# The mask products of three attentions: issued once per bank of scores and ahead of them, with one set of score products for both branches of the sparse attention

## The chip, the cores and the metric

One core of a Trainium2 chip runs the whole program. The metric is the time on the device, in microseconds; of the kernel before there are three runs, with a median of 2802.47 us (2797.93 to 2806.33).

The core's engines work side by side, each from its own queue: TensorE (PE in the profile; its loads of weights, PEld) multiplies matrices, VectorE (DVE) and ScalarE (ACT) work element by element and reduce, GpSimd (POOL) takes a few such steps, SyncE (SP) issues most of the transfers. TensorE writes to PSUM, eight banks of 128 rows by 512 fp32 numbers. A product there has a stationary operand, which is loaded first, and a moving one, whose columns stream through.

## The reference, cut to what matters

256 tokens of width 1024 pass through two blocks of two layers each. Three of the four mixers are attentions, and a causal mask belongs to each score before its softmax:

```python
# _diff_attention, 8 heads of 2 components, 64 wide
sc = jnp.einsum('bqhcd,bkhcd->bhcqk', qb, kb).astype(f32) * scale
sc = jnp.where(mask, sc, -jnp.inf)
...
# nsa_mixer (sparse attention), 16 heads in 4 key groups: the selected and the window branch
p_s = masked_softmax(s_s.reshape(...), m_s)
p_w = masked_softmax(jnp.einsum('bgrqd,bgkd->bgrqk', qb, kw), m_w)
...
# fox_mixer, 16 heads, with the forget gates' running sums c
s = jnp.einsum('bhqd,bhkd->bhqk', qb, k).astype(jnp.float32) + cb[..., None] - c[:, :, None, :]
p = masked_softmax(s, pos[None, :] <= t[:, None])
```

With 256 tokens, the window and the selected blocks of the sparse attention both cover all keys up to the query, so both branches have the same mask. The other layers (a gated MLP, feed-forward layers, two layers of 16,384 experts each) are dense products with weights that are read once.

## The kernel before, in words

The tokens are two tiles of 128, t = 0 and 1. Products in fp32 are made of three float32r products each: an operand is split into a high and a low part, and `mm3` (lines 254 to 258) adds high by high, low by high and high by low in one accumulation. Weights come in blocks of 128 by 1024: SyncE loads them, ScalarE and VectorE split them (lines 248 and 249), TensorE multiplies (lines 397 and 469 with 512 columns, `lin_b` through `mm3` with 256).

The schedule is written by hand: each engine gets its instructions in the order in which the Python code issues them. In an attention, `attend` (line 899) runs over units. A unit is two sets of scores that share one PSUM bank, each 128 queries by kn keys, where kn is 128 for tile 0 and 256 for tile 1. In the differential attention (`unit`, line 1049) and in fox (`unit`, line 1705) the two sets are two heads, 8 units per tile; in the sparse attention (`nsa`, `unit`, line 1491) they are one head's selected and window branch, 16 units per tile. Each tile has two banks for its scores, used in turn. The parts of a unit trail one another by the steps that `ORDER` (line 50) gives: `scores`; `peak`, the row maxima by VectorE (line 958); `soft`, the exponentials by ScalarE (line 965); `scale`; `turn`, the transposes by TensorE (lines 1098, 1543, 1742) and their split; `pv`, the product with v. So the scores of unit i can only be written once the exponentials of unit i - 2 have been read out of the bank. `weave` (line 911) mixes the units of both tiles with blocks of the product before ("c") and of the one after ("w"), in the order of the strings `FILL` (line 52).

The mask is added by TensorE. `maskb` holds 0 or -1e30 in bfloat16, `identb` the identity; the product of the two, 128 columns, is added to the last 128 keys of each set of scores, after them, and closes the set's accumulation (lines 1064, 1506 and 1723). In the sparse attention the code before is

```python
for b in range(2):
    p = self.A[t].halves[i % 2][:, b * S:b * S + kn]
    self.mm3(p, [x[rr, h // 2, ts_] for x in qT], [x[rr, b, g, :kn] for x in kT], True, False)
    nc.tensor.matmul(p[:, kn - P:], self.identb, self.maskb, start=False, stop=True)
```

The queries are the stationary operand, the keys the moving one; `rr` takes 64 rows, those of one head, so a score product uses 64 of TensorE's 128 rows while the mask product and the transposes use all. In fox a fourth product per set, over 4 rows (line 1722, `cx`), adds the running sums. The maxima of a unit wait for its last product, before the change a mask product.

Of the kernel before, what the change touches and what calls it, by code (L numbers as in the profile page):

```python
# [59 lines left out]
def ffn_ops():  # L60
    """The pairs of up blocks ("u") and the down blocks ("d") in their order."""
    ops = [("u", 4)] + [("d", f) for f in range(4)] + [("u", 5)] + [("d", f) for f in range(4, 8)]
    for k in range(6, 14):
        ops += [("u", k), ("d", 2 * k - 4), ("d", 2 * k - 3)]
    return ops + [("u", 14), ("u", 15)] + [("d", f) for f in range(24, 32)]
# [5 lines left out]
class Stream:  # L71
    """The weights, block by block: a load, then the two float32r parts in a slot."""
# [9 lines left out]
    def aside(self, key):  # L82
        """True for the blocks whose second part GpSimd makes."""
# [8 lines left out]
    def open(self, pool, n):  # L92
        """n more slots, for the blocks that the plan lets use them."""
        self.free += [self._slot(pool, self.k.nm("x"), True) for _ in range(n)]
# [18 lines left out]
    def _one(self):  # L113
        """Splits the next block, if there is room for it."""
# [56 lines left out]
class Wide:  # L171
    """[128, 1024] in two banks of PSUM, of which one can be written while the other is read."""
# [15 lines left out]
class Build:  # L188
# [17 lines left out]
    def tick(self):  # L206
        """One step of each task."""
# [14 lines left out]
    def begin(self, task):  # L222
        """A task whose first step goes out at once."""
# [6 lines left out]
    def need(self, t):  # L230
        """The input of a stage, tile t."""
# [22 lines left out]
    def mm3(self, out, s, m, start, stop):  # L254
        mm = self.nc.tensor.matmul
        mm(out, s[0], m[0], start=start, stop=False)  # L256
        mm(out, s[1], m[0], start=False, stop=False)  # L257
        mm(out, s[0], m[1], start=False, stop=stop)  # L258

    def ps(self, shape):  # L260
        """The next bank of the ring, as a shape."""
# [22 lines left out]
    def rstd(self, ms, eps, table=True, beside=None, r=None):  # L284
        """(ms + eps) ** -0.5, by ScalarE's table or, to leave its tables alone, by GpSimd; ms may be in two parts.

        beside() goes out while it is on its way."""
# [20 lines left out]
    def load_table(self, func):  # L308
        """ScalarE's table of func, ahead of its use."""
# [12 lines left out]
    def transpose_split(self, src, dst, c0, n, tsl, scale=None):  # L322
        """src [128 tokens, n*128]: chunks c0.. of dst[hi/lo][:, c, tsl]."""
# [8 lines left out]
    def wait(self, n):  # L332
        """Steps in which weights aren't split."""
# [5 lines left out]
    def turn_raw(self, t, xt, wait):  # L339
        """h's tile t, transposed and split into xt, without the norm's gain (the weights have it) and its r."""  # L340
# [6 lines left out]
    def turn_normed(self, t, g, xt, wait, table, part):  # L347
        """rmsnorm of h's tile t, transposed and split into xt; the last norm without xt."""
# [11 lines left out]
    def chain(self, t, m, post, pre, xt, wait=5, table=True):  # L360
        """h += m, or its rmsnorm; then the next stage's norm, with its gain pre or raw."""
# [25 lines left out]
    def block(self, key, c, x, t, out, ws, ncols, start, stop):  # L387
        """out[:, n] (tokens of tile t) += x^T w over row chunk c."""
# [13 lines left out]
    def ahead(self, keys, x, after=None, ncols=1024, start=True, stop=True):  # L402
        """Steps of a product for tile 0; those for tile 1 are put off."""
# [14 lines left out]
    def late(self):  # L418
        """The next block put off; False without one."""
# [18 lines left out]
    def linear(self, keys, x, after=None, ncols=1024, start=True, stop=True, lag=LAG, func=None):  # L438
        """A product for both tiles, tile 1 LAG blocks behind; after(t) once tile t is done.

        Towards the end tile 1 falls up to lag blocks behind, to be done beside what follows for tile 0, and func's
        table is loaded."""
# [13 lines left out]
    def lin_b(self, key, x, out):  # L456
        """out [n, tokens] of one block [128, 8, n]."""
# [134 lines left out]
    def open_side(self, n_gain):  # L592
        """What all but the expert layers use besides: a second input, slots of the stream, gains."""
# [7 lines left out]
    def dump(self, stage):  # L601
        """Ends the program after a stage, for tests of a part."""
# [42 lines left out]
    def load_x(self):  # L645
        """The input, the first weights before and between its tiles."""
# [4 lines left out]
    def load_p(self, i, also=None):  # L651
        """The layer's p, transposed, in two parts."""
# [8 lines left out]
    def proj(self, i, c, t, pt, ws):  # L661
        """pp = p w_proj, row chunk c of tile t."""
# [6 lines left out]
    def gmlp(self, xt, yt):  # L669
        nc, tc, a = self.nc, self.tc, self.a  # L670
        with tc.tile_pool(name="gm", bufs=1) as gp:
# [55 lines left out]
            def spatial():  # L727
                """s + b of all groups; u s of tile 0."""
# [46 lines left out]
    def ffn(self, i, xr, xt, also=None):  # L775
        """xr holds the raw input, xt will hold the normed one, xr the next stage's."""
# [72 lines left out]
    def scaled(self, x, t):  # L849
        """x = A[t] times the norm's r."""  # L850
# [3 lines left out]
    def inverse(self, t):  # L854
        """1 / r as a row."""
# [8 lines left out]
    def ple(self, i, xt, nxt):  # L864
# [11 lines left out]
        def mid(t, c):  # L876
            """The bias over r, that the sigmoid's scale takes back."""
# [21 lines left out]
    def attend(self, n, order, **parts):  # L899
        """Steps over n units: each one's parts trail one another, as far as order says.  # L900

        s: the scores; m: their maxima; e: the exponentials; c: the scale; t: the transposes and their first part;
        l: the second one; p: the product with v."""
# [7 lines left out]
    def weave(self, order, units, join, make):  # L911
        """The steps of both tiles' units (0, 1), those of tile 1's product before (c) and of tile 0's after (w).

        join(t) ends what tile t's units need, before the first of them or where order has z (0) or u (1); make begins
        the product after."""
# [39 lines left out]
    def maxima(self, s, n):  # L955
        """The negated row maxima of the score sets s [128, n, kn]."""
# [4 lines left out]
    def exps(self, s, n, kn, e, nm):  # L961
        """e = exp of the score sets s [128, n, kn] plus nm; the rows' sums."""
# [5 lines left out]
    def low(self, parts):  # L968
        """The second part of what the first was copied from."""
# [7 lines left out]
    def normed(self, e, r, kn, engine):  # L977
        """e [128, 2, kn] times r [128, 2]."""
# [1150 lines left out]
```

## Time and profile before

| what | value |
|---|---|
| runs | 2797.93, 2802.47, 2806.33 us (median 2802.47) |
| profiled execution | span 2807.0 us, on one core; nothing else of its time is listed |
| mean granted TensorE clock | 0.964 of full speed |
| TensorE busy | 2721.5 us, 97% of the span |
| VectorE, ScalarE, GpSimd busy | 73%, 48%, 5% |
| DMA | 448 MB, 160 GB/s on average |

The profile tells one execution. It lists the busy time of each engine, groups of instructions with their mean duration, the waits, and a timeline in which each line has a start and a duration. The ends of matmuls are modelled, because they are pipelined: a product's record lasts longer than the distance to the next start, and it is the distances between starts that add up to time. The granted clock is TensorE's, as a share of 2.4 GHz: 1.00 or 0.50 at any moment, and a mean of the two in a stretch.

### The profile page before, as it was taken

To read this page: it belongs to the slowest core of one execution; us is meant where nothing else is said; L and a number is where in the kernel's file an instruction comes from. 1 tells how busy PE (TensorE), PEld (TensorE's weight loads), DVE (VectorE), ACT (ScalarE), POOL (GpSimd) and SP (SyncE) were. 2 spreads that over 40 slices of the span, in tenths; PEclk is the share of its full clock that TensorE was granted. 3 is DMA by queue.
4 is the path that set the end of the run, shared out by engine and by line. 5 is a ranking of instruction groups with operands and counts; after the bars stand their busy time and mean duration, and the time that the engine had idled before them with its cause. 6 is when DMAs were issued, how large, how long until landed. Compare 5 with 4: busy or idle time off the path is not lost.

```text
span 2807.0 us, 44583 instructions
## 1 busy us (share of the span) xinstructions
PE 2721.5 (97%) x17590; PEld 2355.8 (84%) x17590; DVE 2043.0 (73%) x3492; ACT 1337.9 (48%) x2056; POOL 141.0 (5%) x130
## 2 busy tenths in 40 slices
PE   8999999999879999999999999999999999999998
PEld 6789777898657799999977788777899999877887
DVE  5655766656764579988899965455699888899664
ACT  5544654545443444444444454353554444444553
POOL 2200020000122100000000000010000000000000
PEclk9999997999986999999999999997999999999999
DMA  6655551554450146665555576440456655555663
GB/s 209 183 187 187 170 162 55 185 190 147 153 179 9 39 151 188 180 181 173 168 162 169 170 218 196 145 146 29 135 178 185 186 170 171 165 166 172 207 207 118
DMA packets 125237, 448.43 MB, mean 160 GB/s; under 512 B 15058, under 2 KB 15586, under 8 KB 125028
## 3 DMA queue, kind: packets, MB, share of 16 engines
q1 hardware_dynamic: 122404, 437.45, 50.7%
q0 software_dynamic: 2624, 8.14, 1.0%
q8 instruction: 137, 2.24, 0.3%
q14 instruction: 72, 0.59, 0.1%
HBM read 444.49 MB, written 1.05 MB: 159 GB/s over the span
## 4 chain that ended last, share of the span: by engine, by line
PE 32%; issue 31%; DVE 3%; ACT 1%; DMA 1%; POOL 0%; DVEq 0%; POOLq 0%; ACTq 0%
PE A L469 12%; PE B L256 4%; PE B L258 4%; PE B L257 4%; PE A L397 4%; PE B L1953 1%; DVE lob L249 1%; PE A L256 1%; PE A L1722 0%; PE B L1742 0%; PE A L257 0%; PE A L258 0%; PE B L1543 0%; PE A L1723 0%; DMA trir<-in_c_tri 0%
## 5 line engine op out<-in xcount | busy, mean ns | idle before, releaser
L248 ACT CAST hib<-raw 128x1024 fp32r<-128x1024 f32 x519 | 543.3, 1050 | 716.7 <-PE B L258 344.5
L249 DVE TENSOR_TENSOR lob<-raw,hib 128x1024 fp32r<-128x1024 f32 x508 | 618.5, 1220 | 189.9 <-ACT hib L248 189.3
L256 PE MATMUL B<-xa,hib 128*128 128x256 f32 x2096 | 593.1, 283 | 0.0
L257 PE MATMUL B<-xa,lob 128*128 128x256 f32 x2096 | 588.1, 281 | 0.1
L258 PE MATMUL B<-xa,hib 128*128 128x256 f32 x2096 | 587.2, 280 | 0.0
L469 PE MATMUL A<-hib,xa 128*128 128x512 f32 x1440 | 412.7, 400 | 4.9 <-ACT xa L248 4.9
L257 PEld LDWEIGHTS B<-xa,lob 128*128 128x128 f32 x2096 | 394.9, 188 | 1.2 <-DVE lob L249 0.6
L256 PEld LDWEIGHTS B<-xa,hib 128*128 128x128 f32 x2096 | 394.7, 188 | 0.0
L258 PEld LDWEIGHTS B<-xa,hib 128*128 128x128 f32 x2096 | 394.5, 188 | 0.0
L469 PEld LDWEIGHTS A<-hib,xa 128*128 128x128 f32 x1440 | 266.5, 189 | 65.8 <-ACT xa L248 5.2
L249 DVE TENSOR_TENSOR lox<-raw,hix 128x1024 fp32r<-128x1024 f32 x174 | 211.2, 1226 | 130.3 <-ACT hix L248 129.9
L248 ACT CAST hix<-raw 128x1024 fp32r<-128x1024 f32 x192 | 197.7, 1043 | 159.2 <-PE A L469 53.1
L469 PE MATMUL A<-lob,xa 128*128 128x512 f32 x720 | 227.4, 397 | 0.0
L1960 DVE SCALAR_TENSOR_TENSOR H<-B,H 128x512 f32<-128x512 f32 x128 | 169.6, 1328 | 1.0 <-PE B L1953 0.6
L397 PE MATMUL A<-hix,xb 128*128 128x512 f32 (+1 forms) x520 | 161.1, 409 | 4.9 <-DVE nv L252 4.2
L469 PEld LDWEIGHTS A<-lob,xa 128*128 128x128 f32 x720 | 135.6, 188 | 32.7
L469 PE MATMUL A<-hix,xa 128*128 128x512 f32 x480 | 133.3, 395 | 0.0
L252 DVE SCALAR_TENSOR_TENSOR lox<-raw,gcol,hix 128x1024 fp32r<-128x1024 f32 (+1 forms) x75 | 93.2, 1250 | 42.8 <-ACT hix L251 42.7
L397 PE MATMUL A<-hix,xa 128*128 128x512 f32 x400 | 121.3, 405 | 1.1 <-ACT hix L251 1.1
L397 PEld LDWEIGHTS A<-hix,xb 128*128 128x128 f32 x520 | 98.6, 198 | 26.0 <-DVE nv L252 4.8
L469 PEld LDWEIGHTS A<-hix,xa 128*128 128x128 f32 x480 | 90.0, 187 | 22.0
L249 DVE TENSOR_TENSOR xa<-H,xa 128x256 fp32r<-128x256 f32 x256 | 106.7, 420 | 0.9 <-ACT xa L248 0.9
(502 smaller groups left out, 4798.3 us busy)
## 6 DMA issues: line engine op xcount, KB each, us to landing
raw<-in_u SPq DMA_DIRECT2D x256, 512.0 KB, 3.6
raw<-in_v SPq DMA_DIRECT2D x256, 512.0 KB, 3.7
raw<-in_f_w_down SPq DMA_DIRECT2D x64, 512.0 KB, 3.5
raw<-in_w_up SPq DMA_DIRECT2D x48, 512.0 KB, 4.4
raw<-in_l_w_in SPq DMA_DIRECT2D x40, 512.0 KB, 3.6
raw<-in_b_w_qkv SPq DMA_DIRECT2D x24, 512.0 KB, 4.5
raw<-in_a_w_in SPq DMA_DIRECT2D x16, 512.0 KB, 4.2
raw<-in_f_w_up SPq DMA_DIRECT2D x16, 512.0 KB, 3.6
```

Of the source, the lines that this page charges most:

```text
L248: nc.scalar.copy(hi, src)
L249: engine.tensor_tensor(lo, src, hi.bitcast(F32), op=ALU.subtract)
L252: nc.vector.scalar_tensor_tensor(lo, src, scale, hi.bitcast(F32), op0=ALU.mult, op1=ALU.subtract)
L256: mm(out, s[0], m[0], start=start, stop=False)
L257: mm(out, s[1], m[0], start=False, stop=False)
L258: mm(out, s[0], m[1], start=False, stop=stop)
L397: self.nc.tensor.matmul(out[:, n0:n0 + n], xs[u], w[v][:, n0:n0 + n], start=start and i == 0, stop=stop and i == 2)
L469: self.nc.tensor.matmul(self.A[t][:, n0:n0 + 512], x[u][:, ts_], w[v][:, n0:n0 + 512], start=first and q == 0, stop=last and q == 2)
L1953: nc.tensor.matmul(p[:, t, :], A[:, t].rearrange("p a b -> p (a b)"), B[q][:, t].rearrange("p a b -> p (a b)"), start=q == 0, stop=q == 1)
L1960: nc.vector.scalar_tensor_tensor(hv, p, 1.0 / G_SCALE, hv, op0=ALU.mult, op1=ALU.mult)
```

## The change

A helper `masked` adds the mask to both sets of a bank in one product of 256 columns: its moving operand is `maskb` read twice, and its output is the last 128 keys of both sets. It is issued ahead of the unit's score products, and it, no longer the first score product, starts the accumulation. The score products only add; the last of them ends the unit. In the sparse attention one `mm3` takes the keys of both branches at once, 2 kn columns instead of kn, so that there are three score products in a unit instead of six. In fox the two products with the running sums come right behind the mask, ahead of both heads' scores. The number of mask products falls from 32 to 16 in the differential attention, from 64 to 32 in the sparse one and from 32 to 16 in fox. Comments are dropped as well.

```diff
-    def mm3(self, out, s, m, start, stop):
+    def mm3(self, out, s, m, start, stop, **kw):
...
+    def masked(self, sets):
+        kn = sets.shape[2]
+        self.nc.tensor.matmul(sets[:, :, kn - P:], self.identb, self.maskb[:, None, :].to_broadcast([P, 2, P]),
+                              start=True, stop=False, skip_group_check=True)
...
                 def scores(i):                                  # differential attention
                     r = slice(i % 2 * 64, i % 2 * 64 + 64)
+                    self.masked(banks[i % 2][:, :, :kn])
                     for e in range(2):
                         h = i // 2 * 2 + e
-                        p = banks[i % 2][:, e]
-                        self.mm3(p[:, :kn], [x[r, h, ts_] for x in qkT[0]], [x[r, h, :kn] for x in qkT[1]], True,
-                                 False)
-                        nc.tensor.matmul(p[:, kn - P:kn], self.identb, self.maskb, start=False, stop=True)
+                        self.mm3(banks[i % 2][:, e, :kn], [x[r, h, ts_] for x in qkT[0]],
+                                 [x[r, h, :kn] for x in qkT[1]], False, True, skip_group_check=True)
...
                     rr = slice((h % 2) * 64, (h % 2) * 64 + 64)  # sparse attention
-                    for b in range(2):
-                        p = self.A[t].halves[i % 2][:, b * S:b * S + kn]
-                        self.mm3(p, [x[rr, h // 2, ts_] for x in qT], [x[rr, b, g, :kn] for x in kT], True, False)
-                        nc.tensor.matmul(p[:, kn - P:], self.identb, self.maskb, start=False, stop=True)
+                    self.masked(sets(i))
+                    self.mm3(sets(i), [x[rr, h // 2, ts_] for x in qT], [x[rr, :, g, :kn] for x in kT], False, True,
+                             skip_group_check=True)
...
                     r = slice(64 * b, 64 * b + 64)               # fox
+                    self.masked(banks[b][:, :, :kn])
+                    for e in range(2):
+                        h = 2 * (i // 2 * 2 + e) + b
+                        k4 = 32 * (h // 4 % 2 * 2 + b)
+                        k4, sl = slice(k4, k4 + 4), h // 8 * 2 + e
+                        mm(banks[b][:, e, :kn], cx[k4, 0, sl, ts_], cx[k4, 1, sl, :kn], start=False, stop=False,
+                           skip_group_check=True)
                     for e in range(2):
                         g = i // 2 * 2 + e
-                        h = 2 * g + b
-                        o = banks[b][:, e, :kn]
-                        k4 = 32 * (h // 4 % 2 * 2 + b)
-                        k4, sl = slice(k4, k4 + 4), h // 8 * 2 + e
-                        self.mm3(o, [x[r, g, ts_] for x in qT], [x[r, g, :kn] for x in kT], True, False)
-                        mm(o, cx[k4, 0, sl, ts_], cx[k4, 1, sl, :kn], start=False, stop=False)
-                        mm(o[:, kn - P:], self.identb, self.maskb, start=False, stop=True)
+                        self.mm3(banks[b][:, e, :kn], [x[r, g, ts_] for x in qT], [x[r, g, :kn] for x in kT], False,
+                                 True, skip_group_check=True)
```

## Rows read from the trace of the kernel before

**Rows 1.** Page: busy time, share of the span, instructions, of each engine.

```profile
PE 2721.5 (97%) x17590; PEld 2355.8 (84%) x17590; DVE 2043.0 (73%) x3492; ACT 1337.9 (48%) x2056; POOL 141.0 (5%) x130
```

**Rows 2.** Windows: span, busy (count) of PE, PEld, DVE, ACT, POOL; granted clock, DMA.

```profile
415.00:456.00 41.00, 37.38 (x153) 30.70 (x153) 23.90 (x65) 15.24 (x55) 7.05 (x5) 0.50 0.09 26
829.00:903.00 74.00, 68.49 (x305) 56.81 (x304) 40.16 (x103) 27.54 (x99) 20.06 (x22) 0.56 0.10 35
903.00:950.00 47.00, 43.96 (x309) 36.51 (x308) 26.56 (x71) 25.25 (x83) 14.51 (x16) 1.00 0.00 1
1903.00:1941.00 38.00, 38.00 (x142) 28.98 (x142) 18.83 (x43) 13.81 (x51) 2.35 (x1) 0.51 0.04 15
```

**Rows 3.** Waits of PE in 829 to 952 us: total us, times, longest.

```profile
PE A L256 <- ACT e L965: 3.2, 3, 1.2
```

**Rows 4.** PE timeline, sparse attention, tile 0: start, duration, line, operands.

```profile
861.92 0.47 PE L256 MATMUL A<-nkT,xa 64*128 64x128 f32 x1
862.19 0.42 PE L257 MATMUL A<-nkT,xa 64*128 64x128 f32 x1
862.41 0.41 PE L258 MATMUL A<-nkT,xa 64*128 64x128 f32 x1
862.75 0.29 PE L1506 MATMUL A<-maskb,identb 128*128 128x128 bf16 x1
862.97 0.47 PE L256 MATMUL A<-nkT,xa 64*128 64x128 f32 x1
...
863.89 0.64 PE L1531 MATMUL B<-ident,scr 128*128 128x128 f32 x2
```

**Rows 5.** The same timeline, tile 1 (256 columns), the unit before.

```profile
859.60 0.58 PE L256 MATMUL A<-nkT,xa 64*128 64x256 f32 x1
859.98 0.41 PE L257 MATMUL A<-nkT,xa 64*128 64x256 f32 x1
...
860.76 0.58 PE L256 MATMUL A<-nkT,xa 64*128 64x256 f32 x1
```

**Rows 6.** PE timeline, 512 columns in the differential attention.

```profile
410.68 1.05 PE L397 MATMUL A<-lox,xb 128*128 128x512 f32 x2
411.53 0.66 PE L397 MATMUL A<-hix,xb 128*128 128x512 f32 x2
```

**Rows 7.** PE timeline: the product with v, then scores.

```profile
865.82 0.41 PE L258 MATMUL B<-pt,nv 128*128 128x256 f32 x1
866.16 0.47 PE L256 MATMUL A<-nkT,xa 64*128 64x128 f32 x1
```

**Rows 8.** PE timeline, full clock: a unit of tile 0.

```profile
914.32 0.32 PE L256 MATMUL A<-nkT,xa 64*128 64x128 f32 x1
...
915.51 0.39 PE L1543 MATMUL B<-ident,e 128*128 128x128 f32 x2
```

**Rows 9.** PE groups by shape, 903 to 950 us: count, busy, mean ns.

```profile
L258 PE MATMUL A<-nkT,xa 64*128 64x256 f32 x18 | 5.1, 284 | 0.0
...
L258 PE MATMUL A<-nkT,xa 64*128 64x128 f32 x6 | 1.6, 272 | 0.0
```

**Rows 10.** PE timeline, fox, tile 1.

```profile
1929.16 0.58 PE L256 MATMUL A<-fkT,xa 64*128 64x256 f32 x1
...
1930.10 0.57 PE L1722 MATMUL A<-fcx 4*128 4x256 f32 x1
1930.60 0.29 PE L1723 MATMUL A<-maskb,identb 128*128 128x128 bf16 x1
1930.82 0.58 PE L256 MATMUL A<-fkT,xa 64*128 64x256 f32 x1
```

**Rows 11.** PE groups by shape, 1903 to 1941 us.

```profile
L1722 PE MATMUL A<-fcx 4*128 4x256 f32 x12 | 6.9, 575 | 0.0
```

**Rows 12.** PE groups by shape, 415 to 456 us.

```profile
L256 PE MATMUL A<-qk,qk 64*128 64x256 f32 x14 | 8.0, 574 | 0.0
```

**Rows 13.** PE, split moving operand: count, ns min/median/max, first, last start.

```profile
L258 PE MATMUL B<-gvn,ws x8: 281/283/283, 67.8 to 70.3; 128*128 128x256 f32 x8
```

More of the change, by code (lines that the diff above doesn't have):

```diff
@@ L252, in split @@
             nc.vector.scalar_tensor_tensor(lo, src, scale, hi.bitcast(F32), op0=ALU.mult, op1=ALU.subtract)
-    def mm3(self, out, s, m, start, stop):
+    def mm3(self, out, s, m, start, stop, **kw):
         mm = self.nc.tensor.matmul
-        mm(out, s[0], m[0], start=start, stop=False)
-        mm(out, s[1], m[0], start=False, stop=False)
-        mm(out, s[0], m[1], start=False, stop=stop)
+        mm(out, s[0], m[0], start=start, stop=False, **kw)
+        mm(out, s[1], m[0], start=False, stop=False, **kw)
+        mm(out, s[0], m[1], start=False, stop=stop, **kw)
+    def masked(self, sets):
+        kn = sets.shape[2]
+        self.nc.tensor.matmul(sets[:, :, kn - P:], self.identb, self.maskb[:, None, :].to_broadcast([P, 2, P]),
+                              start=True, stop=False, skip_group_check=True)
     def ps(self, shape):
```

## The prediction, made before the change was run

> **What bounds the kernel now.** I read the page first: TensorE is busy 97% of the span, no other engine over 73% [rows 1]. A modelled busy share alone doesn't make a bound, so next came the windows of the three attentions [rows 2]. Two things are to be seen there. TensorE is busy for 37.4 of 41 us, 68.5 of 74, 44.0 of 47 and 38.0 of 38, while VectorE and ScalarE stand near a half. And TensorE's clock is granted at 0.50, 0.56 and 0.51 in three of these stretches, 1.2 GHz nearly all the time, while the sparse attention's end, from 903 us, runs at 1.00. DMA is at 0.00 to 0.10: the loads are ahead and wait for slots. Third the waits: in the whole sparse attention TensorE waits 3.2 us, three times, for the exponentials that free a bank of scores [rows 3]. So in these 200 us the order on TensorE sets the pace: what its products no longer take, the end no longer takes, as long as the softmax keeps up.
>
> **The steps of a unit at half clock.** Last came the timeline, where distances between starts count. In a branch of 128 columns [rows 4] first to second score product is 0.27 us, second to third 0.22, third to mask 0.34, mask to the next first product 0.22: 1.05 in all. A unit up to its transposes is 863.89 - 861.92 = 1.97; its second branch is 0.13 shorter, since transposes follow a mask sooner than scores do. With 256 columns [rows 5] first to second is 0.38 and a branch 1.16, so 0.11 more: the first product's added columns are seen, those of the others are hidden behind the loads. A unit of tile 1 is 2 x 1.16 - 0.13 = 2.19. What costs is the change between 64 and 128 rows: 0.34 against 0.22 for the same third product. A product of 512 columns takes 0.85 / 2 = 0.43 [rows 6].
>
> By the Trainium skill (TensorE: Matmul & The Clock Gate, the mechanism of part 3) a load overlaps a running product only when their row groups differ. Here the rows say the reverse: 0.22 between products of the same 64 rows, 0.34 where rows change. By that rule the 32 places where the second head's scores now follow the first's would cost 0.34, not 0.22, and the gain below would be 3 us less; the trace disagrees, and I go by the rows.
>
> **Sparse attention.** Removed per unit: three score products, one mask product, two row changes. New order: mask with 256 columns to first score, 0.22 + 0.11 = 0.33; then tile 0: 0.38 (256 columns), 0.22, 0.34 to what follows, together 1.27 against 1.97, saves 0.70. Tile 1: first to second 0.38 + 0.21 for 256 more columns = 0.59, then 0.43, then 0.34 + 0.21 = 0.55, together 1.90 against 2.19, saves 0.29. Ahead of a unit, scores now start 0.34 after a product with v [rows 7]; a mask there is a step without a change of rows. No row shows that step. It can't be longer than the 0.34 into a mask with a change of rows [rows 4], so nothing is lost and perhaps nothing saved; nor shorter than the 0.22 - 0.13 = 0.09 with which transposes follow a mask, so at most 0.25 is saved. I take 0.13, the 0.34 turned into 0.21, as between products of one row count, which it is nearest to. So 0.83 and 0.42 at half clock. At full clock the unit of tile 0 is 1.19 [rows 8], 0.60 of 1.97, and I scale both: 0.50 and 0.25. After 903 us 18 products of 256 columns and 6 of 128 remain at each place [rows 9], two to a unit: 9 units of tile 1 and 3 of tile 0. The other 7 and 13 lie before, 88% at half clock (0.56 = 0.88 x 0.5 + 0.12). Tile 0: 11.4 x 0.83 + 4.6 x 0.50 = 11.8. Tile 1: 6.2 x 0.42 + 9.8 x 0.25 = 5.0. Sum **16.8**.
>
> **Fox.** A head of tile 1 takes 1930.82 - 1929.16 = 1.66, of which 0.50 is the product of 4 rows up to the mask [rows 10]; a unit 3.32 - 0.13 = 3.19. After: mask 0.33, the two 4-row products 0.38 and 0.34 (as a first and a last product of one row count), then 0.38, four times 0.22, 0.34: 2.65. Saves 0.54, with the 0.13 ahead 0.67. Tile 0, by 0.11 less where the columns are seen: 2.75 against 2.43, with the 0.13 0.45. 12 heads of tile 1, 6 units, ran at half clock [rows 11]; the rest I count at full: 6 x 0.67 + 2 x 0.40 + 8 x 0.27 = **7.0**.
>
> **Differential attention.** Tile 1: mask 0.33, 0.38, four times 0.22, 0.34 = 1.93 against 2.19; 0.26 + 0.13 = 0.39. Tile 0: 0.33 + 0.27 + 0.88 + 0.34 = 1.82 against 1.97; 0.28. 14 heads, 7 units, ran at half clock [rows 12]: 7 x 0.39 + 0.23 + 8 x 0.17 = **4.3**.
>
> **What lies beside.** No instruction of SP, POOL, VectorE or ScalarE is added, removed or moved past another; no DMA is issued elsewhere. The wait for a free bank moves from the first score product to the mask; the same products stand behind it on TensorE. VectorE's maxima wait for the last score product, which is now what ends the unit, at the 0.34 counted. The reordering of fox's small products costs nothing by itself: their operands are made before the first unit. What is late next is the softmax: where TensorE runs at full clock it waits already [rows 3], and a shorter unit leaves less time to maxima and exponentials. I take the 3.2 us to double: -3.2.
>
> 16.8 + 7.0 + 4.3 - 3.2 = 24.9. The profiled execution has a span of 2807.0; it would become 2782.1. The median of the runs is 4.5 lower, so 2802.5 - 24.9 = 2777.6. Ends: with nothing saved ahead of the masks (64 units, about 0.1 each) 6.5 less, with 0.25 6 more; with half of all full-clock savings (some 10 us) lost to waits 2 us less. So 2770 to 2787 for this case.
>
> **Rivals.** (a) *The clock comes back earlier in the sparse attention.* The half-clock stretch has units of 128 columns, the full-clock one mostly 256 [rows 2, 9], TensorE being 93% busy in both. Afterwards every unit streams the same columns in less time, with fewer loads. That speaks for it; against it, fox's scores of 256 columns were slow too [rows 11]. Some 65 us of the 74 are at half clock; 12 fall away by the sum, of the other 53 half would go at most. Half of that gained: 13 us more, 2765; all: 2751.
>
> (b) *The softmax takes TensorE's place.* If half of the saving only became waits for exponentials, 12.5 us: 2790. Against it: VectorE is busy 40 of 74 us, ScalarE 28 [rows 2].
>
> (c) *Outputs in two runs are slow.* The masks write two runs of 128 numbers in a bank, tile 0's merged scores too; no row shows such an output. If each took its columns' time twice: 64 masks by 0.16 (0.21 at half clock, 0.11 at full) and 48 score products by 0.18, 18.9 us: 2796.5, not measurably changed. Split moving operands, at least, run at (70.3 - 67.8) / 21 = 0.12 a product of 256 columns [rows 13], with 21 starts between first and last of eight by three: no slower than a whole one. The Trainium skill (PSUM, specifications) says of this that any non-contiguous access pattern slows matmuls significantly; for moving operands the trace doesn't agree, for outputs nothing here shows it.
>
> (d) *Slower: the end of the sparse attention loses its clock.* From 903 us TensorE is busy 44 us at full clock [rows 2]. If shorter bursts and longer waits for exponentials there bring the half clock that ruled before, the 44 us, less some 5 saved, take up to twice the time: 39 - 25 = 14 us slower, 2816. It decides once more than 25 us of full-clock work falls to half. Against it: nothing but gaps is taken out, and waits are 3.2 us in 121.
>
> That the change does not do what it says is no case of weight: the orders are written out, so 64 masks and 96 score products must be missing from TensorE's 17590.
>
> **Numbers.** Forecast 0.48; (a) 0.30; (b) 0.10; (c) 0.07; (d) 0.05. A measurement of this kernel can tell about 0.3%, 8.4 us, from no change. Faster by more are the forecast, (a) and most of (b), 0.08 of 0.10: 0.86; within it (c) and the rest of (b): 0.09; slower: 0.05. The range reaches from the deep end of (a) to (b): 2752 to 2794, where a little over half of the saving is lost; it leaves out (c), (d) and the last of (a).
>
> **What would show it.** Right: 17430 matmuls; 0.33 from mask to first score at half clock and about 1.3 for a unit of tile 0; the sparse attention some 14 us shorter, fox 7, the differential 4, all else unmoved; PE still near 93% busy. Wrong: a mask of two runs that takes over 0.4 at half clock (c); waits for exponentials over 10 us (b); a granted clock in the 829 to 903 stretch well over 0.56 (a), or after it under 1.00 (d).

## The result, and the profile after

The changed kernel took 2765.48 us (median of 4 runs, 2761.11 to 2768.64) against 2802.97 of the kernel before (4 runs, 2797.93 to 2806.33): a ratio of 0.9867, with a 95% interval of 0.985 to 0.9885. It is 37.5 us faster, 1.3%. The forecast was 25 us; the time lies in the range of 2752 to 2794, below the 2770 to 2787 of the forecast's own case and near the 2765 worked out for rival (a).

The page of the kernel after: span, then busy time, share and instructions of each engine.

```profile
span 2762.7 us, 44255 instructions
...
PE 2677.4 (97%) x17430; PEld 2320.0 (84%) x17430; DVE 2035.7 (74%) x3492; ACT 1337.3 (48%) x2056; POOL 142.2 (5%) x130
```

TensorE has 160 products fewer, 17430 for 17590 [rows 1], as the orders say: 64 masks and 96 scores. Its share of the span is 97% as before. Line numbers have moved by 6 to 8: the mask is now line 265, the exponentials 973, the transposes of the sparse attention 1549, those of fox 1750.

To compare the attentions I take the stretch from the first to the last score product of each: the differential attention, the sparse one, fox. Columns: length, busy us (count) of PE, PEld, DVE, ACT, POOL, then the granted clock, the DMA share and GB/s. The windows of the kernel before:

```profile
392.24:444.94 52.70, 50.42 (x219) 39.09 (x219) 31.51 (x70) 25.05 (x78) 15.29 (x7) 0.68 0.25 81
829.31:936.62 107.31, 100.14 (x527) 82.66 (x527) 60.27 (x159) 47.08 (x167) 31.45 (x35) 0.70 0.07 24
1877.13:1942.72 65.59, 65.59 (x275) 49.88 (x276) 35.49 (x69) 28.88 (x89) 14.28 (x6) 0.69 0.20 65
```

The same windows of the kernel after:

```profile
387.56:437.66 50.10, 47.48 (x203) 38.65 (x203) 29.23 (x69) 24.73 (x78) 15.49 (x7) 0.66 0.27 84
821.67:906.99 85.32, 77.20 (x399) 59.06 (x399) 59.18 (x157) 46.44 (x167) 31.45 (x35) 0.79 0.08 26
1844.66:1899.78 55.12, 52.71 (x260) 42.68 (x259) 31.79 (x69) 28.66 (x88) 14.72 (x6) 0.78 0.26 77
```

The three are 2.6, 22.0 and 10.5 us shorter, 35.1 together. These are two single executions, whose spans differ by 44.3 us (2807.0 and 2762.7); of the 9.2 us beyond the stretches 4.7 lie ahead of the first score product, where nothing was changed. The column to see is the clock. At two levels, a mean of 0.70 over 107.31 us is 64 us at half clock (twice the length times what is missing to 1), and 0.79 over 85.32 is 36. In fox 41 us became 24, in the differential attention 34 stayed 34. So TensorE does its steps in less time, and it also spends 45 us less at 1.2 GHz.

The steps themselves, in the timeline of PE in the kernel after (start, duration, line, operation, operands, count), at half clock: a product of 128 rows, a unit of tile 0 up to its transposes, and one of tile 1 up to the next mask.

```profile
843.28 0.37 PE L258 MATMUL B<-kc,xa 128*128 128x32 f32 x1
843.50 0.40 PE L265 MATMUL A<-maskb,identb 128*128 128x256 bf16 x1
843.83 0.58 PE L256 MATMUL A<-nkT,xa 64*128 64x256 f32 x1
844.21 0.41 PE L257 MATMUL A<-nkT,xa 64*128 64x256 f32 x1
844.42 0.41 PE L258 MATMUL A<-nkT,xa 64*128 64x256 f32 x1
844.76 0.69 PE L1549 MATMUL B<-ident,e 128*128 128x128 f32 x2
...
848.13 0.42 PE L265 MATMUL A<-maskb,identb 128*128 128x256 bf16 x1
848.48 0.79 PE L256 MATMUL A<-nkT,xa 64*128 64x512 f32 x1
849.07 0.62 PE L257 MATMUL A<-nkT,xa 64*128 64x512 f32 x1
849.50 0.62 PE L258 MATMUL A<-nkT,xa 64*128 64x512 f32 x1
850.06 0.40 PE L265 MATMUL A<-maskb,identb 128*128 128x256 bf16 x1
```

Mask to first score 0.33 and 0.35, first to second 0.38 and 0.59, second to third 0.21 and 0.43, third to what follows 0.34 and 0.56: 1.26 and 1.93, where the prediction had 1.27 and 1.90 for the 1.97 and 2.19 of before. Into the mask from a product of 128 rows it is 843.50 - 843.28 = 0.22, where 0.21 was assumed.

The first line of a unit of tile 1 and the line right behind the unit, in the differential attention and in fox, also at half clock:

```profile
427.36 0.44 PE L265 MATMUL A<-maskb,identb 128*128 128x256 bf16 x1
...
429.30 0.47 PE L256 MATMUL B<-xa,at 128*128 128x128 f32 x1
...
1874.20 0.42 PE L265 MATMUL A<-maskb,identb 128*128 128x256 bf16 x1
...
1876.85 0.69 PE L1750 MATMUL B<-ident,e 128*128 128x128 f32 x2
```

That is 1.94 and 2.65 us, where the prediction had 1.93 and 2.65.

The loads tell of the rule weighed in the prediction once more: third score product after second, same 64 rows, 0.21; transposes after the third, rows changed, 0.34. Where the second head's scores follow the first's, the step is 0.22 in the differential attention (428.32 to 428.54 us) and 0.21 in fox (1875.87 to 1876.08). That a load overlaps only where row groups differ (the Trainium skill, TensorE: Matmul & The Clock Gate, the mechanism of part 3) is not what this trace shows, at any of these places.

Waits of PE in the kernel after, in the sparse attention's stretch (total us, times, longest):

```profile
PE A L265 <- ACT e L973: 3.5, 4, 1.2
```

The same in fox's stretch:

```profile
PE B L1750 <- DVE e L989: 1.4, 1, 1.4
PE A L265 <- ACT e L973: 0.8, 1, 0.8
```

In the sparse attention the wait for exponentials, now in front of the mask, is 3.5 us; it was 3.2 [rows 3]. In fox 2.2 us are new: once the transposes wait for the normalised exponentials, once a mask for exponentials. A wait of 3.4 us for VectorE early in the sparse attention, which [rows 3] don't show, stayed, with 3.3 us.

### The profile page after: what moved, and what is told of

It is laid out like the page before. It is cut to its first block, busy times and chain, and to the rows that moved or that the text cites. A ratio compares the mean times of both kernels' runs of the same rounds, so it can differ in the third digit from the quotient of the medians.

```text
span 2762.7 us, 44255 instructions
## 1 busy us (share of the span) xinstructions
PE 2677.4 (97%) x17430; PEld 2320.0 (84%) x17430; DVE 2035.7 (74%) x3492; ACT 1337.3 (48%) x2056; POOL 142.2 (5%) x130
## 4 chain that ended last, share of the span: by engine, by line
PE 31%; issue 31%; DVE 4%; ACT 1%; DMA 1%; POOL 0%; DVEq 0%; POOLq 0%; ACTq 0%
PE A L477 12%; PE B L256 4%; PE B L258 4%; PE B L257 4%; PE A L405 4%; PE B L1961 1%; DVE lob L249 1%; PE A L256 0%; DVE xb L249 0%; PE B L1750 0%; PE B L1549 0%; ACT e L973 0%; DMA raw<-in_wq 0%; PE B L336 0%; DVE pt L979 0%
## 5 line engine op out<-in xcount | busy, mean ns | idle before, releaser
L477 PEld LDWEIGHTS A<-hib,xa 128*128 128x128 f32 x1440 | 266.5, 189 | 65.6 <-ACT xa L248 5.2
```

What stands on the lines that cost most here:

```text
L477: self.nc.tensor.matmul(self.A[t][:, n0:n0 + 512], x[u][:, ts_], w[v][:, n0:n0 + 512], start=first and q == 0, stop=last and q == 2)
```

## The experiments

All times are medians beside runs of the kernel before on the same chip. "At half clock" is for the whole program and worked out from each run's span and mean granted clock, twice the span times what the clock lacks to 1, as a mean over the runs, with the least and the most.

| kernel | time, us | before, us | ratio, 95% interval | at half clock, us |
|---|---|---|---|---|
| before (16 runs beside e1 to e4) | 2801.9 | | | 198 (179 to 213) |
| changed | 2765.5 | 2803.0 | 0.9867 (0.985 to 0.9885) | 149 (138 to 155) |
| e1, scores merged only | 2781.6 | 2801.9 | 0.9933 (0.9909 to 0.9957) | 162 (139 to 184) |
| e2, masks only | 2778.2 | 2801.9 | 0.9927 (0.9902 to 0.9952) | 171 (155 to 189) |
| e3, sparse attention as before | 2791.7 | 2801.9 | 0.9963 (0.9949 to 0.9977) | 183 (161 to 196) |
| e4, sets side by side | 2772.9 | 2801.9 | 0.9907 (0.9883 to 0.9931) | 157 (144 to 172) |
| e5, mask twice | 2770.7 | 2803.2 | 0.9891 (0.9867 to 0.9915) | 148 (138 to 161) |
| e6, one added product | 2777.4 | 2803.2 | 0.9905 (0.9871 to 0.9938) | 143 (122 to 161) |
| e7, two added products | 2770.0 | 2803.2 | 0.9895 (0.9865 to 0.9924) | 100 (83 to 128) |
| e8, mask last | 2764.6 | 2803.2 | 0.9863 (0.9841 to 0.9886) | 141 (127 to 149) |
| e9, two added, fox alone | 2764.6 | 2802.7 | 0.9859 (0.9838 to 0.9881) | 135 (132 to 138) |
| e10, two added, not in the sparse attention | 2758.1 | 2802.7 | 0.9839 (0.9821 to 0.9857) | 99 (94 to 105) |
| e11, changed kernel again | 2767.3 | 2802.7 | 0.9874 (0.9853 to 0.9894) | 147 (144 to 155) |
| e12, two masks ahead | 2769.9 | 2799.8 | 0.989 (0.9875 to 0.9906) | 149 (138 to 161) |

The first theory is the prediction's: the steps on TensorE set the time, at whatever clock a stretch had before. The rival is (a): the change also brings the clock back. The first four kernels take the change apart.

**e1: the merged scores alone.** The kernel before, but for the sparse attention's scores:

```diff
-                    for b in range(2):
-                        p = self.A[t].halves[i % 2][:, b * S:b * S + kn]
-                        self.mm3(p, [x[rr, h // 2, ts_] for x in qT], [x[rr, b, g, :kn] for x in kT], True, False)
-                        nc.tensor.matmul(p[:, kn - P:], self.identb, self.maskb, start=False, stop=True)
+                    self.mm3(sets(i), [x[rr, h // 2, ts_] for x in qT], [x[rr, :, g, :kn] for x in kT], True, False,
+                             skip_group_check=True)
+                    for b in range(2):
+                        nc.tensor.matmul(sets(i)[:, b, kn - P:], self.identb, self.maskb, start=False, stop=True,
+                                         skip_group_check=True)
```

> Only the sparse attention's score products are merged; each set keeps its own mask product behind the scores, and the differential attention and fox are as before. Steps alone (the clock's shares as before): tile 0 saves 0.38 + 0.22 + 0.34 + 0.11 + 0.08 = 1.13 against 1.97, so 0.84 a unit at half clock, tile 1 about 0.4, together 14 us less than before, the sparse attention near 93 us from first to last score product. Clock as well: as in the changed kernel, about 85 us from first to last score product, 22 us less than before, with some 35 us at half clock instead of 65. If it needs the mask ahead: no more than 7 us less.

The windows of the sparse attention and of fox, first to last score product (columns as above):

```profile
821.62:911.99 90.37, 79.16 (x431) 61.86 (x430) 61.67 (x165) 47.43 (x171) 32.93 (x36) 0.75 0.10 36
1851.84:1914.31 62.47, 61.73 (x275) 46.90 (x276) 34.76 (x71) 29.77 (x92) 14.47 (x6) 0.75 0.22 68
```

2781.6 us, 20 less than before (the runs reach from 2775.1 to 2791.1): nearer to the 22 of the clock than to the 14 of the steps. The sparse attention has 17 of it: 90.4 us, between the 93 and 85 expected, and at half clock for 45 of them instead of 64. Of the 90.4, 6.7 us are waits for VectorE early in the stretch, which take 3.3 in the changed kernel. Nothing of the gain needs the mask ahead. Fox, whose instructions are those of before, took 62.5 us here, with 31 us at half clock, against 65.6 and 41 in the profile of before: so much it scatters without a change of its own.

**e2: the masks alone.** The changed kernel, with two sets of three products again in the sparse attention:

```diff
                     self.masked(sets(i))
-                    self.mm3(sets(i), [x[rr, h // 2, ts_] for x in qT], [x[rr, :, g, :kn] for x in kT], False, True,
-                             skip_group_check=True)
+                    for b in range(2):
+                        self.mm3(sets(i)[:, b], [x[rr, h // 2, ts_] for x in qT], [x[rr, b, g, :kn] for x in kT], False,
+                                 True, skip_group_check=True)
```

> Masks ahead and one per bank everywhere, fox reordered, but the sparse attention's scores in two sets of three products. Steps alone: differential attention 4, fox 7, sparse attention 32 units of about 0.3 at a mean clock, 8: 19 us less than before. Clock as well: fox 12 less, because its clock comes back as in the changed kernel; in the sparse attention about 60 of its 100 us stay at half clock, since the six score products stay, so the sparse attention gains only its 8; about 23 us less than before.

Windows of the differential and the sparse attention:

```profile
387.33:429.19 41.86, 36.89 (x204) 29.42 (x203) 28.97 (x69) 24.61 (x78) 15.55 (x7) 0.89 0.33 101
814.03:916.75 102.72, 96.32 (x496) 82.51 (x495) 59.15 (x157) 46.77 (x167) 31.46 (x35) 0.66 0.06 22
```

2778.2 us, 24 less. The sparse attention is only 5 us shorter than before, at 0.66 and so with 70 us at half clock: with six score products to a unit its clock doesn't come back, though a unit changes rows only twice here, as in the changed kernel. The total meets the 23 us of the expectation by other parts: the sparse attention gave 5 where 8 were expected, fox 9 (56.5 us) where 12 were. A surprise is the differential attention, whose instructions are those of the changed kernel: 41.9 us at 0.89 here, 50.1 at 0.66 there. The same code runs in one or the other, as the clock has it.

**e3: the differential attention and fox alone.** The sparse attention's `scores` is that of the kernel before.

> The sparse attention as before, the differential attention and fox as changed. Steps alone: 4 + 7 = 11 us less than before. Clock as well: fox 12, differential attention 3: 15 us less. In both the sparse attention keeps 107 us from first to last score product and about 65 us at half clock.

Windows of the sparse attention and fox:

```profile
819.99:932.38 112.39, 105.62 (x527) 87.22 (x527) 60.30 (x159) 47.16 (x167) 31.43 (x35) 0.65 0.06 22
1874.56:1929.67 55.11, 52.51 (x259) 42.70 (x259) 31.80 (x69) 28.20 (x87) 14.74 (x6) 0.78 0.25 77
```

2791.7 us, 10 less: the 11 of the steps, not the 15 of the clock. Fox takes 55.1 us at 0.78, as in the changed kernel, so its time comes from its own part. How much of its gain is clock isn't settled: against the fox of e1 it is 7.4 us, not 10.5. The sparse attention, unchanged, took 5 us more than in the profile of before, at 0.65: that much a profile scatters in one stretch by its clock alone, and a part's gain of 5 us can't be read from one profile.

**e4: one run instead of two.** Rival (c) is tried with tile 0's two sets side by side:

```diff
-                    return self.A[t].halves[i % 2].rearrange("p (b k) -> p b k", b=2)[:, :, :kn]
+                    return self.A[t].halves[i % 2][:, :2 * kn].rearrange("p (b k) -> p b k", b=2)
```

> The changed kernel with the two sets of a unit of tile 0 of the sparse attention side by side in the bank, so that masks and scores of that tile write one run of 256 numbers. If outputs in two runs cost nothing: the time of the changed kernel, within 2 us, and 0.33 us from mask to first score at half clock as there. If they cost their columns' time again: 14 us less than the changed kernel, and about 0.22 there.

A unit of tile 0 at half clock, in the timeline of PE:

```profile
843.72 0.40 PE L265 MATMUL A<-maskb,identb 128*128 128x256 bf16 x1
844.04 0.58 PE L256 MATMUL A<-nkT,xa 64*128 64x256 f32 x1
844.42 0.42 PE L257 MATMUL A<-nkT,xa 64*128 64x256 f32 x1
844.64 0.41 PE L258 MATMUL A<-nkT,xa 64*128 64x256 f32 x1
844.98 0.69 PE L1549 MATMUL B<-ident,e 128*128 128x128 f32 x2
```

The steps are those of two runs, to a hundredth: 0.32, 0.38, 0.22, 0.34. The sparse attention's stretch took 85.44 us (85.32 in the changed kernel). The whole was 2772.9 us: not the 14 us faster of rival (c), but 7 more than the changed kernel's 2765.5 (8.5 by the runs of before beside each), outside the 2 us expected. Half-clock time was 157 us against 149, worth some 3 us; the rest isn't explained. In these steps outputs in two runs of 128 numbers cost nothing. The Trainium skill (PSUM — Partial Sum Buffer, Specifications) says that any non-contiguous access pattern slows matmuls significantly; for these runs of 512 bytes the trace doesn't agree.

e5 to e7, and e9 and e10 after them, ask what the clock follows. Added products are the lever: they only cost time if the clock doesn't move.

**e5: the mask twice.** In `masked`, the product is issued two times.

> The changed kernel with every mask product issued twice (the second starts the accumulation anew, so the first has no effect). It adds 64 products of 256 columns: 0.11 us each at full clock, 0.21 at half. Steps alone (granted clock unmoved): 7 us more counted at full clock, 9 to 10 us slower than the changed kernel, low-clock time in the attentions up by about 6 us. Clock follows how densely TensorE streams: the 7 us of full-clock work stay, but the time at half clock falls by 10 us or more, so that the run is at most 2 us slower or faster.

2770.7 us, 3 to 5 more than the changed kernel (2765.5 and, in e11, 2767.3), with 148 us at half clock. The time lies between the two expectations; the 10 us less at half clock, the sign of the clock's case, did not come.

**e6 and e7: added products of 512 columns.** Ahead of each unit's `masked`, one or two times:

```diff
+            self.nc.tensor.matmul(bank.rearrange("p (a k) -> p a k", a=4), self.identb,
+                                  self.maskb[:, None, :].to_broadcast([P, 4, P]), start=True, stop=False,
+                                  skip_group_check=True)
```

> The changed kernel with one product of 512 columns (identity by the mask in bfloat16, into the unit's own bank ahead of its mask, which overwrites it) added to each of the 64 units: 0.21 us each at full clock, 14 us in all. Steps alone: 14 us at full clock, about 20 us slower than the changed kernel. Clock by density: time at half clock in the three attentions, 94 us in the changed kernel's profile, falls below 60, which gives back 17 us or more; same time or faster.

> The same with two such products per unit, 27 us of full-clock work. Steps alone: about 40 us slower than the changed kernel. Clock by density: time at half clock in the attentions near 0, which gives back up to 47 us; between 20 us faster and 5 us slower.

One product per unit: 2777.4 us (2767.5 to 2784.1), 10 to 12 more, less than the 20 that the steps give, more than the clock's case allowed. Two: 2770.0 us, 27 us of added full-clock work for 3 to 5 us of time, with 100 us at half clock instead of 149. The windows of e7, differential attention, sparse attention, fox:

```profile
386.75:432.65 45.90, 43.48 (x233) 31.22 (x233) 28.82 (x71) 24.51 (x77) 15.50 (x8) 0.90 0.28 92
813.92:913.90 99.98, 91.27 (x462) 62.60 (x461) 61.62 (x162) 46.55 (x166) 32.07 (x36) 0.81 0.09 31
1853.19:1902.80 49.61, 48.58 (x289) 36.27 (x289) 32.97 (x68) 28.37 (x87) 14.62 (x6) 1.00 0.26 85
```

Fox runs at 1.00 throughout and takes 49.6 us, less than the 55.1 of the changed kernel, though 32 more products were issued in it. The differential attention is at 0.90 and 45.9. The sparse attention doesn't follow: 0.81, some 38 us at half clock as without them, and 14.7 us longer. So the clock's case held for the time, and for two of the three stretches.

**e8: the mask last.** One product per bank, but behind the scores:

```diff
-                    self.masked(sets(i))
-                    self.mm3(sets(i), [x[rr, h // 2, ts_] for x in qT], [x[rr, :, g, :kn] for x in kT], False, True,
-                             skip_group_check=True)
+                    self.mm3(sets(i), [x[rr, h // 2, ts_] for x in qT], [x[rr, :, g, :kn] for x in kT], True, False,
+                             skip_group_check=True)
+                    self.masked(sets(i))
```

The same in the other two; there the second head's scores follow the first's, and the mask (in fox the two products of 4 rows, then the mask) closes the unit.

> The changed kernel with the one mask product per bank behind the scores instead of ahead (in fox the products of 4 rows come behind the scores too). Steps: a unit has the same two changes between 64 and 128 rows; 0.34 us into the mask takes the place of 0.33 out of it, so the time is that of the changed kernel, within 3 us. If the place ahead is worth something by itself (0.13 us a unit, as forecast): 6 to 8 us slower than the changed kernel.

The timeline of PE at half clock: the last product with v, then a unit of tile 0, then transposes.

```profile
848.48 0.41 PE L258 MATMUL B<-pt,nv 128*128 128x256 f32 x1
848.82 0.58 PE L256 MATMUL A<-nkT,xa 64*128 64x256 f32 x1
849.20 0.41 PE L257 MATMUL A<-nkT,xa 64*128 64x256 f32 x1
849.42 0.41 PE L258 MATMUL A<-nkT,xa 64*128 64x256 f32 x1
849.76 0.40 PE L265 MATMUL A<-maskb,identb 128*128 128x256 bf16 x1
849.95 0.42 PE L1549 MATMUL B<-ident,e 128*128 128x128 f32 x1
```

0.34 into the scores, 0.34 into the mask, 0.19 out of it: from the product with v to the transposes 1.47, and 0.22 + 1.26 = 1.48 with the mask ahead. 2764.6 us, the time of the changed kernel. The place ahead is worth nothing by itself; two changes of rows are paid either way.

**e9 and e10: the added products where they helped.** Two per unit in fox alone, and in fox and the differential attention.

> The changed kernel with the two products of 512 columns in fox's 16 units alone: 7 us of full-clock work. If fox kept its clock only by chance before: 7 us at full clock, about 10 us slower than the changed kernel beside it. If the added products hold the clock: fox near 50 us from first to last score product without half clock, as with the two products everywhere, against 55 in the changed kernel, and 3 to 6 us faster than it.

> The same in the differential attention and fox, 14 us of full-clock work in 32 units. If the clock is held in both: differential attention near 45 us from first to last score product with 10 us at half clock, fox near 50, together 5 to 10 us faster than the changed kernel beside it. If not: 14 to 20 us slower.

**e11: the changed kernel beside them.**

> The changed kernel once more, beside the two others: 2765 us within 5. If the clock's return is chance from run to run rather than the kernel's: time at half clock scattered from 140 to 200 us as before the change; if it is the kernel's: 138 to 160 us in every run, against 180 to 213 before.

2764.6 us with fox alone (2760.8 to 2765.4), 2758.1 with both (2756.4 to 2759.2), 2767.3 for the changed kernel on the same chip (2766.7 to 2768.9). The window of fox in e9:

```profile
1848.58:1899.75 51.17, 50.14 (x290) 37.27 (x289) 33.69 (x70) 29.23 (x90) 14.57 (x6) 0.97 0.26 82
```

The windows of the differential attention and fox in e10:

```profile
392.25:434.71 42.46, 39.80 (x234) 28.41 (x233) 28.08 (x68) 24.15 (x76) 15.32 (x7) 1.00 0.31 100
...
1843.33:1892.92 49.59, 48.56 (x289) 36.29 (x289) 32.98 (x68) 28.37 (x87) 14.60 (x6) 1.00 0.26 84
```

In e10 both stretches are at 1.00 from end to end, 42.5 and 49.6 us. The slowest run of e10, 2759.2, lies under the fastest of the changed kernel, 2761.1 (2766.7 beside it): 9 us are gained by 64 products whose result is thrown away, as the 5 to 10 expected. Fox alone gains 2.6 us, just under the 3 to 6 expected; its slowest run, 2765.4, is faster than the fastest of e11. And the half-clock time of the changed kernel is its own, not chance: 138 to 155 us in all eight runs of the two series, 179 to 236 in the 42 runs of before that stand beside e1 to e12.

**e12: two masks ahead.** In `masked`, one product of 128 columns for each set, the first of them starting the accumulation:

```diff
-        self.nc.tensor.matmul(sets[:, :, kn - P:], self.identb, self.maskb[:, None, :].to_broadcast([P, 2, P]),
-                              start=True, stop=False, skip_group_check=True)
+        for b in range(2):
+            self.nc.tensor.matmul(sets[:, b, kn - P:], self.identb, self.maskb, start=b == 0, stop=False,
+                                  skip_group_check=True)
```

> The changed kernel with two mask products of 128 columns ahead of the scores, one for each set, in place of one of 256. If what costs is the change of rows and not the number of mask products: the second mask follows the first after its own 0.05 to 0.11 us of columns, so the time is that of the changed kernel, within 3 us, with 135 to 160 us at half clock. If a mask product costs its former 0.22 us step at half clock: 64 x 0.1 to 0.2, so 7 to 13 us slower.

Both masks and the first score of a unit of tile 0, in the timeline of PE at half clock (the two masks are one line, x2):

```profile
838.99 0.40 PE L263 MATMUL A<-maskb,identb 128*128 128x128 bf16 x2
839.32 0.58 PE L256 MATMUL A<-nkT,xa 64*128 64x256 f32 x1
```

The two masks take the 0.33 us of the one. 2769.9 us, 2.6 more than e11 on the same chip and so within the 3 us, with 30 us less than the kernel before on its chip, where the changed kernel had 37.5 and 35.5: at most a few us lie in it, and no step shows them. That there are fewer mask products is not what the change gains by.

## Why the prediction was right, and where it fell short

**The bound** was right: TensorE's order sets the pace in the attentions. Shorter steps came out at the end, and nothing outside the attentions took the time back (the stretches are 35.1 us shorter, the runs 37.5).

**The steps** were right, unit by unit: 1.26 and 1.93 us for 1.27 and 1.90 in the sparse attention, 1.94 and 2.65 for 1.93 and 2.65 in the other two, 0.22 ahead of the mask for 0.21. Their causes were those named, the changes of rows (e8, e12: neither the mask's place nor the number of masks matters, as long as a unit changes rows twice instead of four times) and the merged products (e1).

**The waits** were right in size by luck, and wrong in place. The sum gave 3.2 us to the sparse attention, where 0.3 came; in fox 2.2 were new, 1.4 of them not at a bank of scores but ahead of the transposes.

**The step that failed** is the share of half clock: "The other 7 and 13 lie before, 88% at half clock", and the same for fox and the differential attention. The sum went by the clock of before. It can be checked stretch by stretch. A step at full clock takes 0.60 of one at half [rows 4, 8], so each us of half clock that becomes full clock gives 0.4 (an estimate for units of tile 0, used for all).

- Sparse attention: at the old share 64 us of half clock, less the 12 of the sum, would be 52; it was 36. The 16 us are worth 6.4. 16.8 + 6.4 - 0.3 of waits is 22.9; measured 22.0.
- Fox: 41 less 4.9 (the 6 units of 0.67 and some 2 of tile 0) would be 36; it was 24. 12 us are worth 4.8. 7.0 + 4.8 - 2.2 is 9.6; measured 10.5.
- Differential attention: 34 less 2.7 would be 31; it was 34. That costs 1.2. 4.3 - 1.2 is 3.1; measured 2.6.

Together 28.1 of steps, 10.0 of clock, less 2.5 of waits: 35.6 for 35.1 measured. That this fits to half a us is partly luck: each stretch is one profile before and one after, and 0.01 in a mean clock is 2 us of half clock in the sparse attention. The runs bear out the total: half-clock time fell from 198 to 149 us in the mean, 20 of these 49 by the sum's own steps, and the other 29 are worth some 12 us, which gives 37.6 for the 37.5 of the runs. They bear out the place for the sparse attention alone. There the eleven profiles of kernels with merged scores have 34 to 45 us at half clock, the three with six score products to a unit (before, e2, e3) 64 to 79. In fox the 12 us rest on the one profile of before. Against e1's fox, with 31 us, it would be 2, and the ten runs of e3 gained 10.2 us, where the steps less the waits give 9.1.

So the forecast's mechanism held and a rival came on top of it: (a), for which it gave 0.30, and which it saw in the sparse attention alone. Its sign came: the first 74 us of that stretch (821.67 to 895.67) ran at 0.76, where 0.56 stood before. It had been worked out as 13 us for half of the stretch, at 0.5 for each us of half clock; the factor of 0.60 that the prediction used for its steps gives 0.4, and so 10.6. It brought 6 there, and up to 5 came in fox, of which the prediction had said that scores of 256 columns were slow too, as an argument against. That the 2765 of (a) is the time measured is therefore luck.

What brings the clock back is shown by what was done to it, not more. In the sparse attention it is the merge: with six score products per unit it stays at half clock for 64 to 79 us, with three for 34 to 45. Fewer changes of rows alone don't do it there: e2 has two per unit, as the changed kernel, and stood at 70. Whether the merge works through fewer loads, fewer products or longer ones was not tried apart and stays open. With two products of 512 columns more per unit fox loses its half clock (1.00, 0.97 and 1.00 in e7, e9 and e10, 0.81 in e11). The differential attention does so too, by the runs of e10 against those of e9: 99 us at half clock (94 to 105) against 135 (132 to 138). Its profiles alone wouldn't show it, since e2 had it at 0.89 without such products. No single rule comes out of that: the sparse attention of e7 got the same products and kept its 38 us.

**The other rivals.** (b), the softmax as the bound: 2.5 us of it. (c), outputs in two runs: fell in e4. (d), a lower clock at the sparse attention's end: nothing of it, that end ran at 1.00 from 875 us on.

## What to carry to other kernels

Count TensorE's changes between row counts as well as its products: at half clock the step into one took 0.34 us where 0.22 is usual here, and two masks of 128 columns cost no more than one of 256 as long as they stand together. Read the granted clock stretch by stretch before pricing a step, and keep a case for its moving: between a quarter and a third of this gain was clock, by the estimates above. Where TensorE is the bound and stands at half clock, added products are worth a try, stretch by stretch: 14 us of them made this kernel 9 us faster, while in the sparse attention they only cost (15 us in e7).

## What the runs showed of the hardware that was not expected

- Useless work can pay: 64 products of 512 columns more, two in each of 32 units, took the kernel from 2767.3 to 2758.1 us (e10 against e11). The differential attention and fox then ran at 1.00, in 42.5 and 49.6 us. Without them fox took 53.3 to 56.5 us with the same attention code; the differential attention took 41.9 to 50.1.
- Half clock does not double every step. A unit of the sparse attention's tile 0 took 1.97 us at half and 1.19 at full clock, a factor of 1.66.
- The same instructions of one stretch ran at quite different clocks from one kernel to the next: the differential attention of the changed kernel at 0.66, in e2 at 0.89, in e4 at 0.79, with 50.1, 41.9 and 43.9 us. Only the total of several runs told kernels apart.
